# A hybrid decoder step on one core: even and odd columns in separate partitions for the block inverse, and old-state products in pairs

## The chip, the core and the metric

The kernel runs on one core of a Trainium2 chip. The metric is the device time of one execution in microseconds (us). A core has a matrix engine (PE, with its weight loads PEld), three engines for elementwise work (DVE, ACT, POOL) and a queue that issues transfers (SP). Each works through its own instructions in order and waits where an operand isn't ready.

## The reference

One inference step of one decoder layer for 256 prompt tokens and 8 sequences of 8 sample tokens. One input projection feeds a gated delta rule (mixer A) and a sparse attention with an indexer (mixer B); both are projected, gated, merged, projected again and normalised.

```python
h = rms_norm(x, pre_norm_g) * (1.0 + scale) + shift
(a_qkv, a_z, a_b, a_a, b_q, b_k, b_v, b_z, i_q, i_k, i_w, g_a, g_b) = split_columns(h @ w_in)
y_a, s_new, conv_new = gdn_branch(a_qkv, a_z, a_b, a_a, conv_buf, s0, ...)
y_b = attend(q, k, v, qi, i_w, i_k) * silu(b_z)
merged = sigmoid(g_a) * (y_a @ w_pa) + sigmoid(g_b) * (y_b @ w_pb)
return x + gate * rms_norm(merged @ w_out, post_norm_g), ...

# gdn_branch, for chunks of 64 tokens
a_strict = where(strict, (kb @ k.T) * decay, 0.0)
sol = triangular_solve(a_strict, rhs, lower=True, unit_diagonal=True)   # (1 + a_strict)^-1 rhs
u = u_c - w_c @ s                                    # the old state's part
o = qd_c @ s + qk_c @ u
s = s * gt_c + kt_c.T @ u
y = rms_norm(o, gdn_norm_g) * silu(z)
```

The sizes: width 2048, 16 query/key heads and 32 value heads of 128 in mixer A, 16 attention heads.

## The kernel before

All 320 tokens (256 prompt, 64 sample) stand as the moving side of PE, and the weights stream past them. Each weight block of 128x1024 arrives in `raw`, ACT rounds it to `whi`, DVE forms the rest `wlo = raw - whi`, and a main product is the sum of `xh,whi`, `xl,whi` and `xh,wlo`, 8 of each per block, accumulated in a bank `pm`. `whi` and `wlo` have three tiles each.

What else is computed is written as Python generators ("sides"). Between main matmuls a planner runs a round of sides (`side_round`). It keeps its own estimate of when each engine is done (`Clock`), and a side that yields a time is taken up again only when the estimate for PE has passed it: `ready(t)` is the estimate for t to be written, `idle(t)` for t to be written and read, `need(ring)` waits for a free buffer of a ring, and `force(cond)` runs sides until a condition holds. So an edit of a side changes the order of instructions far from it. Nearly all instructions are recorded by one helper and have line L64; they are told apart by the names of their tiles.

In order of time: the adaLN modulation and norm, to about 195 us; attention and indexer with their projections, to 690; gates, to 770; the recurrent stage, to 1650; the branch projections, to 1966; the output projection `stream_out`, to 2092; the last norm, to the end. The recurrent stage has 8 groups of two query/key heads (four value heads). A group has: convolution (`xp`, `cth`, `vf`, transposed by PE `ident,vf` into `vt`), the products `kq_gen`, one `inverse`, one `prompt_chain` and one `sample_chain` for each of its two heads, and a norm (six Squares `ps<-ot` on ACT for each head).

`inverse` inverts the unit triangular matrices of the group: 12 matrices of 128x128, cut into 48 blocks of 32x32 on the diagonal, one in each partition. The block's strict part is loaded into `blk`, `X` starts as the identity, and step j of 31 does two POOL instructions, `tmpx = blk[:, j, j+1:] x X[j, 0:j+1]` and `X[j+1:, 0:j+1] -= tmpx`. A copy puts the transposed inverse in `blk`; both forms are stored to `d_x` and loaded back as parts of `XT`, `X` and `blk`, and PE makes the off-diagonal blocks from them (first `ps<-X,blk`).

`sample_chain` multiplies the old states `S` (8 sequences) with the keys and queries in `R` (`ps<-S,R`, 16 instructions on PE), scales `S` by its decay on POOL (`S<-S,gtr`), subtracts the product from `vt` on DVE, and goes on with `ps<-vt,XT` and `ps<-w,ktok`.

At the end, `scaled(t, p, 3)` takes the sum of squares of the last quarter (ACT Square into `M`) and multiplies it by the gate (DVE); `root(t)` adds up and takes the power -1/2 (DVE, POOL `rs<-rs,mh`); `final(t)` does a multiply and add with the residual for four quarters (DVE) and stores each.

Of the kernel before, what the change touches and what calls it, by code (L numbers as in the profile page):

```python
# [16 lines left out]
D = 2048  # L17
# [212 lines left out]
class Kernel:  # L230
# [933 lines left out]
    def aux_gen(self):  # L1164
# [5 lines left out]
        for t, c0 in enumerate((0, 128, NT)):  # L1170
# [30 lines left out]
        rb = rbt[:, 0:256].rearrange("p (b h) -> p b h", b=NB)  # L1201
        self.tt(rb, self.rowb.rearrange("p (b o) -> p b o", o=1).to_broadcast([128, NB, 32]),
                g[:, 2:3, :].to_broadcast([128, NB, 32]), OP.mult)
        yield self.ready(g, rb)
        yield from self.need(self.ps_side, 2)
        p = self.psum()
        q = self.psum()
# [29 lines left out]
    def token_major(self, src, out_p, out_s, keep=None, keep_s=None):  # L1237

        nc = self.nc
        yield self.ready(src)  # L1240
        yield from self.need(self.ps_side)
        p = self.psum()
        for t in range(3):
            n = 128 if t < 2 else 64
            self.tr(p[:n, 128 * t:128 * t + 128], src[:, 128 * t:128 * t + n])
        if keep is None:
            yield from self.need(self.s_r)
            s = self.s_r.get()
# [12 lines left out]
    def ik_done(self, p):
# [478 lines left out]
    def gdn_open(self):  # L1740
# [15 lines left out]
        self.BT = Ring([a.tile([128, 12, 128], F32, name=f"BT{j}") for j in range(1)])  # L1756
        self.PT = Ring([b.tile([128, 2, 2, 128], F32, name=f"PT{j}") for j in range(3)])
        self.inv = Ring([(a.tile([128, 1024], F32, name="blk"), a.tile([128, 1024], F32, name="X"))])
        self.tmp = a.tile([48, 256], F32, name="tmpx")
        self.XT = Ring([b.tile([128, 12, 128], F32, name=f"XT{j}") for j in range(1)])  # L1760
        for t in self.ct.free:
            nc.gpsimd.memset(t, 0.0)
# [290 lines left out]
    def inverse(self, g, G):  # L2053
# [11 lines left out]
        yield from self.need(self.inv)  # L2065
        tiles = blk, Xt = self.inv.get()
        yield self.idle(blk, Xt)
        nc.sync.dma_start(blk[0:48], d_b.rearrange("k m j i -> (k m) (j i)"))
        nc.gpsimd.memset(Xt[0:48], 0.0)
        nc.gpsimd.memset(Xt[0:48, 0:1024:33], 1.0)  # L2070
        yield
        X = Xt[0:48].rearrange("p (i c) -> p i c", c=32)
        B = blk[0:48].rearrange("p (j i) -> p j i", i=32)
        for j in range(31):
            n, m = 31 - j, j + 1
            t = self.tmp[:, 0:n * m].rearrange("p (i c) -> p i c", c=m)
            bv = B[:, j, j + 1:32].rearrange("p (i o) -> p i o", o=1).to_broadcast([48, n, m])
            xv = X[:, j:j + 1, 0:m].to_broadcast([48, n, m])
            self.tt(t, bv, xv, OP.mult, eng=nc.gpsimd)
            self.tt(X[:, j + 1:32, 0:m], X[:, j + 1:32, 0:m], t, OP.subtract, eng=nc.gpsimd)  # L2080
            if j % 4 == 4 - 1:
                yield self.clock.last - 3.6
        nc.gpsimd.tensor_copy(blk[0:48].rearrange("p (c i) -> p c i", i=32), X.rearrange("p i c -> p c i"))
        yield
        while not self.XT.free:
            yield
# [4 lines left out]
        BO = blk[:, 0:512].rearrange("p (m c) -> p m c", c=64)  # L2091
        BD = blk[:, 512:768].rearrange("p (m c) -> p m c", c=32)
        Q1 = blk[:, 768:1024].rearrange("p (m c) -> p m c", c=32)
        nc.sync.dma_start(d_x[0].rearrange("k m i c -> (k m) (i c)"), Xt[0:48])
        nc.sync.dma_start(d_x[1].rearrange("k m i c -> (k m) (i c)"), blk[0:48])
        yield max(self.clock.last, self.idle(XT))
        nc.gpsimd.memset(XB[0:32, :, 32:64], 0.0)
        nc.gpsimd.memset(XE[32:64, :, 0:32], 0.0)
# [177 lines left out]
    def sample_chain(self, h, G):  # L2276
        nc, i, o = self.nc, self.i, self.o
        e, hv, K = h % 2, 2 * h, self.K[h]
        R = K["R"]
        yield from self.need(self.S)  # L2280
        S = self.S.get()
        yield self.idle(S)
        for v in range(2):
            nc.sync.dma_start(S[:, :, v, :], i["state_gdn"][0, :, hv + v].rearrange("b k v -> k b v"))
        while "T" not in G or "vt" not in K:
            yield
        vt, kt, XT = K["vt"], K["ktok"], G["XT"]
        s, stl = self.scal(G, e)
        yield self.ready(S, vt, XT)
        yield from self.need(self.ps_side)  # L2290
        yield from self.need(self.w)
        xr, wt = vt[:, 2], self.w.get()
        p = self.psum()
        for pp in range(2):
            for j in range(4):
                self.mm(p[32 * j:32 * j + 32, 0:256], R[:, 1 + pp, 32 * j:32 * j + 32], S[:, 2 * j + pp],
                        start=(pp == 0), stop=(pp == 1), skip=True)
        self.R.put(R)
        self.tt(S, S, self.gtr[:, :, hv:hv + 2].rearrange("p b (v o) -> p b v o", o=1).to_broadcast([128, NB, 2, 128]),
                OP.mult, eng=nc.gpsimd)  # L2300
        for v in range(2):
            self.stt(xr[:, v, :], p[:, 128 * v:128 * v + 128], self.neG[:, 2, hv + v:hv + v + 1], vt[:, 2, v, :],
                     OP.mult, OP.add)
        self.ps_side.put(p)
        yield
        yield from self.need(self.ps_side)
        if "ot" not in K:
            yield from self.need(self.ot)
            K["ot"] = self.ot.get()
        ot = K["ot"]  # L2310
        p = self.psum()
        for v in range(2):
            self.mm(p[:, 128 * v:128 * v + 128], XT[:, 8 + 2 * e + v, :], xr[:, v, :])
        self.act(ot[:, 2], p[:, 0:256].rearrange("p (v d) -> p v d", v=2))
        self.tt(wt, p[:, 0:256].rearrange("p (v d) -> p v d", v=2), stl(2), OP.mult)
        self.ps_side.put(p)
        self.drop_T(G)
# [147 lines left out]
        self.flags.add(flag)  # L2465

    def pb_open(self):
        self.force(lambda: self.chains == 16 and len(self.zf.free) == 4 and len(self.w.free) == 6
                   and len(self.gr.free) == 4)
        self.shut("gdnb")  # L2470
        a = self.open("merge", side="right")
        self.M, self.sga, self.sgb = (a.tile([128, KB, NT], F32, name=n) for n in ("M", "sga", "sgb"))
        self.stg.put(a.tile([128, NT], F32, name="stg2"))
        x = a.tile([128, KB, 2, NS], F32R, name="xs")
        self.xs = [x[:, k] for k in range(KB)]

        def gates():
            for src, dst, n in ((self.d_sigb, self.sgb, 10.0), (self.d_siga, self.sga, 20.0)):
                for k in range(0, KB, 2):
                    self.nc.sync.dma_start(dst[:, k:k + 2, :], src[k:k + 2].rearrange("k p t -> p k t"))  # L2480
                    self.gated += 2
                    yield self.later(n if k else 0.0)
        self.gated = 0
        g = gates()
        next(g)
        self.spawn(g, first=True)
        self.pt = Ring([a.tile([128, NT], F32, name=f"pt{j}") for j in range(2)])
        self.spawn(self.load_half(self.d_ya, 0, (self.xh, self.xl), "ya0"))

    def pb_done(self, p, k):  # L2490
        if k == 0:
            self.first = p
            return True
        if k == 1:
            self.pb_open()
            self.ps_main.put(self.psum())
            self.pb_sum(self.first, 0)
            self.ps_main.put(self.first)
        self.pb_sum(p, k)

    def pb_sum(self, p, k):
# [65 lines left out]
    def stream_out(self, u0):  # L2567
# [53 lines left out]
        def sample(p, w, kb, k, **kw):  # L2621
            product(p, self.xs[kb].rearrange("p e t -> p (e t)"), w[:, k], kb, **kw)

        def scaled(t, p, cg):
            c = slice(512 * cg, 512 * cg + 512)
            q = self.sq[t][:, cg:cg + 1]
            if t == 2:
# [76 lines left out]
        scaled(0, p0, 3)
        root(0)
        scaled(2, p, 3)
        root(2)
# [50 lines left out]
```

## Time and profile before

| what | before |
|---|---|
| median of 3 runs | 2102.92 us (2102.68 to 2103.71) |
| profiled execution: its time | 2101.78 us |
| profiled execution: its span | 2100.1 us |
| matmul instructions | 17409 |
| granted clock of PE, mean | 0.999 |
| main memory read | 388.38 MB |
| transferred over the span | 210 GB/s mean |

An instruction row has start and length in us, the engine, the operation, out<-in, the shape and how many follow each other; square brackets name the idle time ahead of it and what ended it. Idle time of an engine off the path costs nothing. The profiled execution's own span leaves out what lies before the first and behind the last instruction, 1.7 us.

### The profile page before, as it was taken

How to read it: one execution, taken by the hardware profiler on the slowest of the kernel's cores; microseconds unless marked ns; L12 is line 12 of the kernel's file. 1: busy time of each engine (PE TensorE's matmuls, PEld its weight loads, DVE VectorE, ACT ScalarE, POOL GpSimd, SP SyncE). 2: the span in 40 equal slices, each digit the busy share in tenths (PEclk: the TensorE clock that was granted, in tenths of full speed). 3: DMA queues.
4: the chain of work that ended last, by engine and by line, in shares of the span. 5: the costliest groups of instructions: out<-in, count | busy, mean ns of one | idle time of the engine just before them, and what ended most of it. 6: DMA issues, size and time to landing. Idle time of an engine off the chain costs nothing.

```text
span 2100.1 us, 44340 instructions
## 1 busy us (share of the span) xinstructions
PE 2080.3 (99%) x17409; PEld 1995.4 (95%) x17409; DVE 1358.0 (65%) x2541; ACT 986.9 (47%) x2213; POOL 567.8 (27%) x768
## 2 busy tenths in 40 slices
PE   8999999999999999999999999999999999999998
PEld 7999999999999999899999999999999999999986
DVE  5676648899855466676777676767666545445543
ACT  4225343333334356574747574747445534333431
POOL 1001000000010118484738383838471000000000
PEclk9999999999999999999999999999999999999999
DMA  9996758885686767696968686868697977575651
GB/s 346 347 345 192 195 146 259 238 261 153 186 260 211 216 164 201 152 257 148 253 160 249 158 242 165 237 163 243 160 260 207 257 208 213 167 182 149 198 193 51
DMA packets 693795, 440.65 MB, mean 210 GB/s; under 512 B 74209, under 2 KB 667985, under 8 KB 691281
## 3 DMA queue, kind: packets, MB, share of 16 engines
q1 hardware_dynamic: 689504, 415.15, 70.2%
q0 software_dynamic: 3616, 21.02, 2.8%
q8 instruction: 137, 2.24, 0.4%
q10 hardware_dynamic: 464, 1.65, 0.2%
q14 instruction: 74, 0.60, 0.1%
HBM read 388.38 MB, written 49.01 MB: 208 GB/s over the span
## 4 chain that ended last, share of the span: by engine, by line
PE 96%; DMA 2%; DVE 1%; issue 0%; ACT 0%; POOL 0%; DVEq 0%; POOLq 0%; ACTq 0%
PE pm L64 70%; PE ps L64 26%; DMA raw<-in_w_ada_dram 1%; DMA rawx<-in_w_ada_dram 1%; DMA c<-in_c_sample_dram 0%; DVE wlo L64 0%; POOL rs L64 0%; DVE awl L64 0%; DVE hT L64 0%; ACT M L64 0%; DVE sgb L64 0%; DVEq L2754 0%; DVE c L64 0%; DVE S L64 0%; DVE sga L64 0%
## 5 line engine op out<-in xcount | busy, mean ns | idle before, releaser
L64 PE MATMUL pm<-xh,whi 128*128 128x320 f32 (+1 forms) x2940 | 888.5, 317 | 0.7 <-DVE qiS L64 0.7
L64 PE MATMUL pm<-xl,whi 128*128 128x320 f32 (+1 forms) x2940 | 859.8, 307 | 0.3 <-DVE xl L64 0.2
L64 DVE TENSOR_TENSOR wlo<-raw,whi 128x1024 fp32r<-128x1024 f32 x446 | 574.8, 1294 | 248.0 <-ACT whi L64 215.8
L64 PEld LDWEIGHTS pm<-xh,whi 128*128 128x128 f32 x2940 | 552.9, 188 | 22.3 <-issue 17.3
L64 ACT ACTIVATE whi<-raw 128x1024 fp32r<-128x1024 f32 x446 | 467.8, 1056 | 192.2 <-PE pm L64 121.0
L64 PEld LDWEIGHTS pm<-xl,whi 128*128 128x128 f32 x2940 | 553.4, 188 | 1.5 <-DVE xl L64 0.7
L64 PE MATMUL pm<-xh,wlo 128*128 128x320 f32 (+1 forms) x2940 | 493.4, 307 | 0.5 <-DVE wlo L64 0.5
L64 PEld LDWEIGHTS pm<-xh,wlo 128*128 128x128 f32 x2940 | 443.8, 188 | 1.0 <-DVE wlo L64 1.0
L64 POOL TENSOR_TENSOR tmpx<-blk,X 48x31 f32<-48x31 f32 (+15 forms) x248 | 167.2, 674 | 45.3 <-DMA blk<-d_b 28.6
L64 POOL TENSOR_TENSOR X<-X,tmpx 48x31 f32<-48x31 f32 (+15 forms) x248 | 172.1, 694 | 19.4
L64 DVE SCALAR_TENSOR_TENSOR ps<-xp,cs,ps 128x344 f32<-128x344 f32 x192 | 111.5, 581 | 35.0 <-ACT ps L64 29.8
L64 POOL TENSOR_TENSOR rs<-rs,mh 128x1 f32<-128x1 f32 (+1 forms) x3 | 4.1, 1366 | 454.6 <-DVE rs L64 454.6
L64 POOL TENSOR_TENSOR S<-S,gtr 128x2048 f32<-128x2048 f32 x16 | 60.9, 3808 | 156.9 <-issue 97.8
L64 PE MATMUL pm<-y1h,whi 128*128 128x320 f32 x336 | 99.4, 308 | 0.0
L64 PE MATMUL pm<-y1l,whi 128*128 128x320 f32 x336 | 99.2, 307 | 0.0
L64 POOL DMA_INDIRECT a<-in_cache_k_dram,idx x8 | 7.5, 938 | 282.8 <-PE ps L64 267.8
L64 ACT ACTIVATE xp<-pm 128x256 f32<-128x256 f32 (+1 forms) x128 | 32.1, 303 | 110.1 <-PE pm L64 110.1
L64 ACT ACTIVATE vt<-ps,sc 128x128 f32<-128x128 f32 (+1 forms) x112 | 39.1, 412 | 54.3 <-PE ps L64 54.2
L64 PEld LDWEIGHTS pm<-y1l,whi 128*128 128x128 f32 x336 | 63.1, 188 | 0.0
L64 PEld LDWEIGHTS pm<-y1h,whi 128*128 128x128 f32 x336 | 62.8, 187 | 0.0
L64 ACT ACTIVATE t<-pm 128x320 f32<-128x320 f32 x36 | 15.9, 441 | 90.3 <-PE pm L64 90.2
L64 PE MATMUL pm<-y1h,wlo 128*128 128x320 f32 x336 | 56.1, 307 | 0.0
(463 smaller groups left out, 3081.7 us busy)
## 6 DMA issues: line engine op xcount, KB each, us to landing
raw<-in_w_in_dram SPq DMA_DIRECT2D x328, 512.0 KB
raw<-in_w_pa_dram SPq DMA_DIRECT2D x64, 512.0 KB
rawx<-in_w_ada_dram SPq DMA_DIRECT2D x18, 1024.0 KB
a<-in_w_ada_dram SPq DMA_DIRECT2D x16, 1024.0 KB
S<-in_state_gdn_dram SPq DMA_DIRECT2D x32, 512.0 KB
out_dram<-S SPq DMA_DIRECT2D x32, 512.0 KB
raw<-in_w_pb_dram SPq DMA_DIRECT2D x32, 512.0 KB
raw<-in_w_out_dram SPq DMA_DIRECT2D x32, 512.0 KB
```

What stands on the lines that cost most here:

```text
L64: made = fn(*args, **kw)
```

## The change

Five places of the program differ.

1. `inverse`: the 32 columns of each block are split; even columns stand in partitions 0 to 47, odd ones in 64 to 111. Each step handles `j // 2 + 1` columns on 112 partitions instead of `j + 1` on 48. `blk` is loaded into both halves; at the end two copies on POOL and two on DVE put the two forms together.
2. `sample_chain`: the first of a group's two chains only enters itself in a list; the second one issues both old-state products into one bank, both `S<-S,gtr` and the four subtractions, and then releases both.
3. `aux_gen` and `token_major`: 2 us are added to a time that is waited for, and a staging buffer is given back 4 us after its estimated last use.
4. `pb_open`, `pb_done`: up to four sums of the attention branch's projection wait in their banks for the end of the last chains, where two did, and the gate tiles for those are loaded without pauses.
5. `stream_out`: `root` comes between the Square and the gate product; `final` takes the quarters in the order 512, 1024, 0, 1536, and for the last 128 prompt tokens the quarter at 0 goes to ACT (Copy with scale) and POOL (add).

```diff
+            yield self.idle(s) + 4.0                  # token_major
             self.s_r.put(s)
...
-        self.tmp = a.tile([48, 256], F32, name="tmpx")
+        self.tmp = a.tile([112, 144], F32, name="tmpx")
...
-        nc.sync.dma_start(blk[0:48], d_b.rearrange("k m j i -> (k m) (j i)"))
-        nc.gpsimd.memset(Xt[0:48], 0.0)
-        nc.gpsimd.memset(Xt[0:48, 0:1024:33], 1.0)
+        for o in (0, 64):
+            nc.sync.dma_start(blk[o:o + 48], d_b.rearrange("k m j i -> (k m) (j i)"))
+        nc.gpsimd.memset(Xt[0:112, 0:512], 0.0)
+        for e, o in enumerate((0, 64)):
+            nc.gpsimd.memset(Xt[o:o + 48, 16 * e:512:33], 1.0)
...
-            n, m = 31 - j, j + 1
+            n, m = 31 - j, j // 2 + 1
...
-        nc.gpsimd.tensor_copy(blk[0:48].rearrange("p (c i) -> p c i", i=32), X.rearrange("p i c -> p c i"))
+        for e, o in enumerate((0, 64)):
+            x = X[o:o + 48]
+            nc.gpsimd.tensor_copy(blk[0:48].rearrange("p (i c e) -> p e i c", c=16, e=2)[:, e], x)
+            nc.vector.tensor_copy(blk[64:112].rearrange("p (c e i) -> p e i c", e=2, i=32)[:, e], x)
...
+        pair = G.setdefault("SR", [])
+        pair.append((hv, R, S, vt))
+        if len(pair) == 2:
+            yield self.ready(XT, *(x for _, _, a, b in pair for x in (a, b)))
+            p = self.psum()
+            for c, (_, r, sv, _) in zip((0, 256), pair):
+                for pp in range(2):
+                    for j in range(4):
+                        self.mm(p[32 * j:32 * j + 32, c:c + 256], r[:, 1 + pp, 32 * j:32 * j + 32], sv[:, 2 * j + pp], ...)
+                self.R.put(r)
+            for c, (h0, _, sv, vv) in zip((0, 256), pair):
+                self.tt(sv, sv, self.gtr[...], OP.mult, eng=nc.gpsimd)
+                for v in range(2):
+                    self.stt(vv[:, 2, v, :], p[:, c + 128 * v:c + 128 * v + 128], ...)
+            G["xr"] = True
+        while "xr" not in G:
+            yield
...
             self.act(out, src, AF.Square, accum_out=q)
+            if then:
+                then(t)
...
-            for c0 in range(0, D, 512):
+            for c0 in (512, 1024, 0, 1536):
...
+                if c0 == 0 and t == 1:
+                    self.act(g, g, AF.Copy, scale=r)
+                    self.tt(g, g, self.resid[t][:, c], OP.add, eng=nc.gpsimd)
+                else:
+                    self.stt(g, g, r, self.resid[t][:, c], OP.mult, OP.add)
```

PE executes the same instructions in number and kind, in another order. On PE, in the first group, the old-state products stood like this before (`ps_` are banks, `vt,XT` and `w,ktok` products of the chains, `X` parts of the inverse):

```order
L64 MATMUL ps_68<-X 64x64
L64 MATMUL ps_69<-XT_7835,X 64x64
L64 MATMUL ps_68<-X 64x64
L64 MATMUL ps_70<-vt_7838,XT_7835 128x128 x2
L64 MATMUL ps_71<-S_7849,R_7811 32x256 x8
L64 MATMUL ps_67<-vt_7839,XT_7835 128x128 x2
L64 MATMUL ps_69<-S_7850,R_7812 32x256 x8
L64 MATMUL ps_68<-w_7840,ktok_7815 128x256
```

and after:

```order
L64 MATMUL pm_65<-xl,whi_79 128x320
L64 MATMUL pm_65<-xh,wlo_82 128x320 x8
L64 MATMUL ps_67<-vt_7840,XT_7837 128x128 x2
L64 MATMUL ps_69<-vt_7841,XT_7837 128x128 x2
L64 MATMUL ps_68<-S_7851,R_7811 32x256 x8
L64 MATMUL ps_68<-S_7852,R_7812 32x256 x8
L64 MATMUL pm_65<-xh,whi_80 128x320
L64 MATMUL pm_65<-xl,whi_80 128x320
```

The two products follow each other into one bank, in every group; in the later groups of before, main matmuls stood between them.

On ACT, in the second group's convolution, the Squares of the two heads of the first group stood like this before (`ps,sc<-ot`; a later instruction scales `ot` in place):

```order
L64 ACTIVATE ps_72<-xp_7803,cs_102 128x344
L64 ACTIVATE ot_7846<-ot_7846,sc_7853 128x128 x6
L64 ACTIVATE ps_70,sc_7853<-ot_7847 128x128 x6
L64 ACTIVATE whi_79<-raw_75 128x1024
L64 ACTIVATE cth_7804<-ps_72 128x344
L64 ACTIVATE whi_80<-raw_75 128x1024
```

and after:

```order
L64 ACTIVATE vt_7840<-ps_67,sc_7854 128x256 x2
L64 ACTIVATE vt_7840<-ps_69,sc_7854 128x256
L64 ACTIVATE xp_7803<-pm_65 128x256
L64 ACTIVATE xp_7803<-pm_65 128x8x8
L64 ACTIVATE xp_7803<-cs_103 128x8x3
L64 ACTIVATE ps_72<-xp_7803,cs_103 128x344
L64 ACTIVATE ps_68,sc_7855<-ot_7848 128x128 x6
L64 ACTIVATE whi_78<-raw_76 128x1024
L64 ACTIVATE ps_71,sc_7856<-ot_7849 128x128 x6
L64 ACTIVATE whi_79<-raw_76 128x1024
L64 ACTIVATE cth_7804<-ps_72 128x344
```

Both heads' Squares now stand between `vt` and `cth`. On PE, the transposes that follow from this `cth` stand behind 48 main matmuls, counted from the transposes that release `vt`. Before, in the same convolution:

```order
L64 MATMUL pm_65<-xl,whi_78 128x320
L64 MATMUL pm_65<-xh,wlo_81 128x320 x8
L64 MATMUL ps_68<-ident,vf_7819 128x128 x2
L64 MATMUL ps_67<-ident,vf_7819 128x128
L64 MATMUL ps_68<-ident,vf_7820 128x128 x2
L64 MATMUL ps_67<-ident,vf_7820 128x128
L64 MATMUL pm_65<-xh,whi_79 128x320
```

and after:

```order
L64 MATMUL pm_66<-xh,wlo_83 128x320 x8
L64 MATMUL ps_70<-ident,ct_7806 128x128
L64 MATMUL ps_67<-ident,vf_7819 128x128 x2
L64 MATMUL ps_69<-ident,vf_7819 128x128
L64 MATMUL ps_67<-ident,vf_7820 128x128 x2
L64 MATMUL ps_69<-ident,vf_7820 128x128
L64 MATMUL pm_65<-xh,whi_78 128x320
```

The transposes of `ct` and `vf` now stand in one burst, half a block earlier against the Squares. At the end of the program DVE had before:

```order
L64 SCALAR_TENSOR_TENSOR sga<-sga,rs_21288,M 128x512 x4
L64 SCALAR_TENSOR_TENSOR sgb<-sgb,rs_21290,sga 64x512 x4
L64 TENSOR_TENSOR sgb<-ps_69,sgb 128x512
L64 TENSOR_SCALAR rs_21289<-sq_21286,rs_21289 128x1
L64 SCALAR_TENSOR_TENSOR sgb<-sgb,rs_21289,M 128x512 x4
```

and after:

```order
L64 SCALAR_TENSOR_TENSOR sga<-sga,rs_21330,M 128x512 x4
L64 SCALAR_TENSOR_TENSOR sgb<-sgb,rs_21332,sga 64x512 x4
L64 TENSOR_SCALAR rs_21331<-sq_21328,rs_21331 128x1
L64 TENSOR_TENSOR sgb<-ps_72,sgb 128x512
L64 SCALAR_TENSOR_TENSOR sgb<-sgb,rs_21331,M 128x512 x3
```

The sum for the root now stands ahead of the gate product, and three quarters are left to DVE.

More of the change, by code (lines that the diff above doesn't have):

```diff
@@ L1203, in aux_gen @@
                 g[:, 2:3, :].to_broadcast([128, NB, 32]), OP.mult)
-        yield self.ready(g, rb)
+        yield self.ready(g, rb) + 2.0
         yield from self.need(self.ps_side, 2)
@@ L1758, in gdn_open @@
         self.inv = Ring([(a.tile([128, 1024], F32, name="blk"), a.tile([128, 1024], F32, name="X"))])
-        self.tmp = a.tile([48, 256], F32, name="tmpx")
+        self.tmp = a.tile([112, 144], F32, name="tmpx")
+        for t in self.inv.free[0]:
+            nc.gpsimd.memset(t, 0.0)
         self.XT = Ring([b.tile([128, 12, 128], F32, name=f"XT{j}") for j in range(1)])
@@ L2067, in inverse @@
         yield self.idle(blk, Xt)
-        nc.sync.dma_start(blk[0:48], d_b.rearrange("k m j i -> (k m) (j i)"))
-        nc.gpsimd.memset(Xt[0:48], 0.0)
-        nc.gpsimd.memset(Xt[0:48, 0:1024:33], 1.0)
+        for o in (0, 64):
[3 more added lines that the diff above has]
+            nc.gpsimd.memset(Xt[o:o + 48, 16 * e:512:33], 1.0)
         yield
-        X = Xt[0:48].rearrange("p (i c) -> p i c", c=32)
-        B = blk[0:48].rearrange("p (j i) -> p j i", i=32)
+        X = Xt[0:112, 0:512].rearrange("p (i c) -> p i c", c=16)
+        B = blk[0:112].rearrange("p (j i) -> p j i", i=32)
         for j in range(31):
-            n, m = 31 - j, j + 1
+            n, m = 31 - j, j // 2 + 1
             t = self.tmp[:, 0:n * m].rearrange("p (i c) -> p i c", c=m)
-            bv = B[:, j, j + 1:32].rearrange("p (i o) -> p i o", o=1).to_broadcast([48, n, m])
-            xv = X[:, j:j + 1, 0:m].to_broadcast([48, n, m])
+            bv = B[:, j, j + 1:32].rearrange("p (i o) -> p i o", o=1).to_broadcast([112, n, m])
+            xv = X[:, j:j + 1, 0:m].to_broadcast([112, n, m])
             self.tt(t, bv, xv, OP.mult, eng=nc.gpsimd)
@@ L2093, in inverse @@
         Q1 = blk[:, 768:1024].rearrange("p (m c) -> p m c", c=32)
-        nc.sync.dma_start(d_x[0].rearrange("k m i c -> (k m) (i c)"), Xt[0:48])
-        nc.sync.dma_start(d_x[1].rearrange("k m i c -> (k m) (i c)"), blk[0:48])
+        nc.sync.dma_start(d_x[0].rearrange("k m i c -> (k m) (i c)"), blk[0:48])
+        nc.sync.dma_start(d_x[1].rearrange("k m i c -> (k m) (i c)"), blk[64:112])
         yield max(self.clock.last, self.idle(XT))
@@ L2288, in sample_chain @@
         s, stl = self.scal(G, e)
-        yield self.ready(S, vt, XT)
-        yield from self.need(self.ps_side)
-        yield from self.need(self.w)
[L2292 to L2305, printed above, removed]
+        xr = vt[:, 2]
+        pair = G.setdefault("SR", [])
+        pair.append((hv, R, S, vt))
+        if len(pair) == 2:
+            yield self.ready(XT, *(x for _, _, a, b in pair for x in (a, b)))
+            yield from self.need(self.ps_side)
+            p = self.psum()
+            for c, (_, r, sv, _) in zip((0, 256), pair):
+                for pp in range(2):
+                    for j in range(4):
+                        self.mm(p[32 * j:32 * j + 32, c:c + 256], r[:, 1 + pp, 32 * j:32 * j + 32], sv[:, 2 * j + pp],
+                                start=(pp == 0), stop=(pp == 1), skip=True)
+                self.R.put(r)
+            for c, (h0, _, sv, vv) in zip((0, 256), pair):
+                self.tt(sv, sv, self.gtr[:, :, h0:h0 + 2].rearrange("p b (v o) -> p b v o", o=1).to_broadcast(
+                    [128, NB, 2, 128]), OP.mult, eng=nc.gpsimd)
+                for v in range(2):
+                    self.stt(vv[:, 2, v, :], p[:, c + 128 * v:c + 128 * v + 128], self.neG[:, 2, h0 + v:h0 + v + 1],
+                             vv[:, 2, v, :], OP.mult, OP.add)
+            self.ps_side.put(p)
+            G["xr"] = True
+            yield
+        while "xr" not in G:
+            yield
+        yield self.ready(xr)
+        yield from self.need(self.w)
+        wt = self.w.get()
         yield from self.need(self.ps_side)
@@ L2467, in pb_open @@
     def pb_open(self):
-        self.force(lambda: self.chains == 16 and len(self.zf.free) == 4 and len(self.w.free) == 6
-                   and len(self.gr.free) == 4)
+        self.force(self.chain_end)
         self.shut("gdnb")
@@ L2475, in pb_open @@
         self.xs = [x[:, k] for k in range(KB)]
+        self.gated = 0
+        opened = len(self.pend)
         def gates():
@@ L2481, in gates @@
                     self.gated += 2
-                    yield self.later(n if k else 0.0)
-        self.gated = 0
+                    if self.gated > opened + 1:
+                        yield self.later(n if k else 0.0)
         g = gates()
@@ L2488, in pb_open, with chain_end @@
         self.spawn(self.load_half(self.d_ya, 0, (self.xh, self.xl), "ya0"))
+    def chain_end(self):
+        return (self.chains == 16 and len(self.zf.free) == 4 and len(self.w.free) == 6 and len(self.gr.free) == 4)
     def pb_done(self, p, k):
         if k == 0:
-            self.first = p
-            return True
-        if k == 1:
-            self.pb_open()
-            self.ps_main.put(self.psum())
-            self.pb_sum(self.first, 0)
-            self.ps_main.put(self.first)
+            self.pend = []
+        if self.pend is not None:
+            self.pend.append((p, k))
+            if len(self.pend) < 4 and not self.chain_end():
+                self.force(lambda: self.ps_side.free)
+                self.ps_main.put(self.psum())
+                return True
+            self.pb_open()
+            pend, self.pend = self.pend, None
+            for b, j in pend:
+                self.pb_sum(b, j)
+                if j < k:
+                    self.ps_main.put(b)
+            return
         self.pb_sum(p, k)
@@ L2622, in sample, with scaled @@
             product(p, self.xs[kb].rearrange("p e t -> p (e t)"), w[:, k], kb, **kw)
-        def scaled(t, p, cg):
+        def scaled(t, p, cg, then=None):
             c = slice(512 * cg, 512 * cg + 512)
@@ L2654, in final @@
             dst = self.o[0][0, 128 * t:128 * t + 128] if t < 2 else self.o[1].rearrange("b t d -> (b t) d")
-            for c0 in range(0, D, 512):
+            for c0 in (512, 1024, 0, 1536):
                 c = slice(c0, c0 + 512)
                 g = self.scaled[t][:, c]
-                self.stt(g, g, r, self.resid[t][:, c], OP.mult, OP.add)
+                if c0 == 0 and t == 1:
[3 more added lines that the diff above has]
+                    self.stt(g, g, r, self.resid[t][:, c], OP.mult, OP.add)
                 nc.sync.dma_start(dst[:, c], g)
@@ L2703, in stream_out @@
             before(t)
[L2704 to L2707, printed above, removed]
+        scaled(0, p0, 3, root)
+        scaled(2, p, 3, root)
         final(0)
@@ L2718, in stream_out @@
         self.force(lambda: not self.sides)
-        scaled(1, p1, 3)
-        root(1)
+        scaled(1, p1, 3, root)
         final(1)
```

## The prediction

> **What bounds the kernel now.** I read the page's busy shares and its chain first, then the busy time by stretches of 100 us, then what TensorE (PE) waited for, and last the single instructions at the places that the change touches.
>
> ```profile
> PE 2080.3 (99%) x17409; PEld 1995.4 (95%) x17409; DVE 1358.0 (65%) x2541; ACT 986.9 (47%) x2213; POOL 567.8 (27%) x768
> PE 96%; DMA 2%; DVE 1%; issue 0%; ACT 0%; POOL 0%; DVEq 0%; POOLq 0%; ACTq 0%
> ```
>
> PE is busy for 2080.3 of 2100.1 us and the chain that ended last is PE for 96%. So only three things move the end: time on PE itself, gaps on PE, and what lies behind its last matmul. The gaps by stretch (the third column is PE's busy time and its matmuls):
>
> ```profile
> 0.00:100.00 100.00, 90.55 (x1132) 84.04 (x1136) 59.96 (x163) 36.15 (x55) 10.18 (x33) 1.00 1.05 349
> 800.00:900.00 100.00, 99.02 (x813) 94.02 (x812) 66.72 (x143) 58.10 (x155) 65.71 (x90) 1.00 0.68 177
> 1500.00:1600.00 100.00, 99.53 (x836) 94.53 (x835) 56.78 (x96) 49.93 (x120) 58.03 (x75) 1.00 0.78 209
> 1700.00:1800.00 100.00, 100.00 (x684) 100.00 (x683) 50.50 (x66) 36.94 (x45) 0.00 (x0) 1.00 0.68 197
> 2000.00:2100.00 100.00, 91.94 (x398) 74.34 (x396) 41.11 (x55) 28.46 (x45) 4.10 (x3) 0.97 0.34 111
> PE ps L64 <- DVE S L64: 0.5, 1, 0.5
> PE ps L64 <- ACT XT L64: 0.5, 1, 0.5
> PE pm L64 <- DVE c L64: 7.5, 2, 7.2
> ```
>
> Start (9.45 us without PE) and end (8.06) are the big gaps; the diff leaves the start alone. In the recurrent stage there are 0.98 us in 800 to 900 and 0.47 in 1500 to 1600, together 1.45. Nothing there waits for POOL. The stretch 1700 to 1800 is full: 684 matmuls in 100 us, 0.146 us for each main matmul (320 columns).
>
> **The change, part by part.**
>
> *Substitution on even and odd columns.* 62 POOL instructions per inverse, eight inverses:
>
> ```profile
> L64 POOL TENSOR_TENSOR tmpx<-blk,X 48x31 f32<-48x31 f32 (+15 forms) x248 | 167.2, 674 | 45.3 <-DMA blk<-d_b 28.6
> L64 POOL TENSOR_TENSOR X<-X,tmpx 48x31 f32<-48x31 f32 (+15 forms) x248 | 172.1, 694 | 19.4
> 1006.55 0.62 POOL L64 TENSOR_TENSOR tmpx<-blk,X 48x256 f32<-48x256 f32 x1
> 1007.24 1.67 POOL L64 TENSOR_TENSOR X<-X,tmpx 48x256 f32<-48x256 f32 x1
> 1253.19 0.23 POOL L64 TENSOR_TENSOR tmpx<-blk,X 48x31 f32<-48x31 f32 x1
> 1253.82 2.08 POOL L64 COPY blk<-X 48x1024 f32<-48x1024 f32 x1
> ```
>
> Before, (167.2 + 172.1) / 8 = 42.4 us per inverse. The slope is (0.62 - 0.23) / 225 elements = 1.7 ns an element. The work falls from 5456 to some 2850 elements per chain of operations, 92 a piece instead of 176: 0.23 + 61 x 0.0017 = 0.33 us each, 21 us for 62. The rows give no price for 112 partitions against 48; I take the same, and 42.4 (no gain) as the other end. Some instructions take 1.0 us more than their length asks (1007.24: 1.67), and that I leave per inverse as it is, some 7 us. So about 28 us, some 14 saved per inverse. On the end this is worth nothing: PE waits for no POOL row, and the planner spends the shorter time by placing later steps earlier. The permuting copy of 2.08 us becomes two of half the size on POOL and two on DVE, which has 35% of its time free: nothing. If that cover were gone, 2 x some 0.6 us would stand ahead of a weight's low half in each group, 10 us in all; the low halves run ahead of PE (the third rival says how far).
>
> The second load of `blk` adds one issue to SP per inverse. The loads behind it:
>
> ```profile
> 1165.16 0.46 SPq L64 DMA_DIRECT2D X<-d_x  x1
> 1167.99 0.69 PE L64 MATMUL ps<-X,blk 32*32 32x32 f32 x32
> ```
>
> One issue is 0.46 us. The last X load left SP at 1165.62 and PE used it at 1167.99, 2.4 us later; 0.46 us fit. In the new order, in the second group, the same product stands behind its loads by less, 0.6 us in main matmuls: a wait from 0 to 2 us there. I take 0.5 for this and the like of it.
>
> *Old-state products in pairs.*
>
> ```profile
> 1071.69 1.07 PE L64 MATMUL ps<-S,R 128*32 128x256 f32 x16
> 1072.69 0.42 PE L64 MATMUL pm<-xh,whi 128*128 128x320 f32 x1
> 1072.94 0.31 PE L64 MATMUL pm<-xl,whi 128*128 128x320 f32 x1
> 1075.97 1.07 PE L64 MATMUL ps<-S,R 128*32 128x256 f32 x16
> 1076.97 0.41 PE L64 MATMUL pm<-xh,whi 128*128 128x320 f32 x1
> ```
>
> Each product takes 1.00 us to the next main matmul, and the first main matmul behind it 0.25 instead of 0.146, 0.10 too much. Paired, one such return falls away per group, 0.8 us in eight; a change of shape at the head, which the rows don't price apart, may save up to 0.15 more, 2.0 us in all. The instructions on PE are the same in number, but other side products have new neighbours too. Between 0 (everything given back by new neighbours; there are 282 bursts of side work instead of 279) and -4.4 (each row of the new order at the mean distance which that pair of kinds has in this trace) I take -3.0, near the pairs' own price with one unit for the neighbours.
>
> *Where the new order makes PE wait.* With both chains of a group released together, both of its norm bursts on ACT come one behind the other, and the next convolution's rows stand behind them.
>
> ```profile
> 994.23 1.21 ACT L64 ACTIVATE vt<-ps,sc 128x256 f32<-128x256 f32 x3 [3.17 <-PE ps L64]
> 996.46 0.26 ACT L64 ACTIVATE ps<-ot 128x128 f32<-128x128 f32 x1
> 998.93 1.04 ACT L64 ACTIVATE whi<-raw 128x1024 fp32r<-128x1024 f32 x1
> 999.88 0.44 ACT L64 ACTIVATE cth<-ps 128x344 f32<-128x344 f32 x1
> 1257.31 1.21 DVE L64 TENSOR_TENSOR wlo<-raw,whi 128x1024 fp32r<-128x1024 f32 x1
> 1287.49 0.54 DVE L64 SCALAR_TENSOR_TENSOR vf<-cth,ps 128x256 f32<-128x256 f32 x2
> 1530.71 0.55 PE L64 MATMUL ps<-ident,vf 128*128 128x128 f32 x3 [0.47 <-DVE S L64]
> ```
>
> After the first group's chains the new ACT order is: `vt`, the convolution's copies, six Squares, `whi`, six Squares, `whi`, `cth`. By the rows: 996.46 - 994.23 = 2.23 to the Squares; 998.93 - 996.46 = 2.47 for six; 0.95 for a `whi`; 2.47 and 0.95 again: 9.07. Then DVE does `wlo` (1.21) and the pair `vf` (0.54): with handovers about 11.0 us after `vt` began. PE releases that `vt` by its transposes and has 48 main matmuls (7.0 us) and some 0.4 us of transposes before it needs `vf`: 7.4. So PE waits 3.6 us, where the longest such wait before was 0.47. Ends: 2.5, if ACT is early at the first Square, and 4.5, if `wlo` is stretched. The waits of before, 1.45 us, stood in the same products at other places and go.
>
> *Store slots, the late sums of the branch projection, gate loads.* They shift transfers and side work in stretches like 1700 to 1800, where PE has no gap to give. Nothing; the bound for moved transfers is one issue, 0.46 us, per step.
>
> *The end.*
>
> ```profile
> 2092.53 0.19 ACT L64 ACTIVATION_READ_ACCUMULATOR M<-ps 128x1 f32 x1
> 2092.76 0.69 DVE L64 TENSOR_TENSOR sgb<-ps,sgb 128x512 f32<-128x512 f32 x1 [2.81 <-ACT M L64]
> 2093.37 0.20 DVE L64 TENSOR_SCALAR rs<-sq,rs 128x1 f32<-128x1 f32 x1
> 2093.65 0.56 POOL L64 TENSOR_TENSOR rs<-rs,mh 128x1 f32<-128x1 f32 x1 [6.47 <-DVE rs L64]
> 2094.25 2.74 DVE L64 SCALAR_TENSOR_TENSOR sgb<-sgb,rs,M 128x512 f32<-128x512 f32 x4 [0.67 <-POOL rs L64]
> ```
>
> All of this is on the path, after PE's last matmul. The power on POOL now runs beside the gate product: 94.25 - 93.65 = 0.60 less. One of four quarters of 0.69 goes to ACT and POOL: at best 0.7 less again, if they work beside DVE. At worst nothing or less, if POOL's add stops DVE:
>
> ```profile
> 1287.06 3.62 POOL L64 TENSOR_TENSOR S<-S,gtr 128x2048 f32<-128x2048 f32 x1 [24.56 <-issue]
> 1287.95 3.82 DVE L64 TENSOR_TENSOR wlo<-raw,whi 128x1024 fp32r<-128x1024 f32 x1
> ```
>
> Here DVE's `wlo`, 1.21 alone, ended 1.09 us after POOL's multiplication had ended: it did nothing until then. POOL's add of a quarter should be a quarter of 3.62 and a base, about 1.0 us. Stopping DVE for that long costs 0.3 more than the quarter that was saved. So the end lies between -1.3 and -0.3; I take -0.6, since this row is the nearest.
>
> The Trainium skill, "SBUF — State Buffer", section "Who interferes with whom", says the same of the end's two operations: a VectorE instruction with two SBUF inputs and a GpSimd instruction that reads SBUF exclude each other for a whole instruction. By it the quarter moved to POOL gains nothing and the end is worth 0.3; without it 1.3.
>
> **Sum.** PE's order -3.0, the new `vf` wait +3.6, other new waits +0.5, old waits -1.45, the end -0.6: -0.95 us. The profiled execution took 2101.78 (its span 2100.1), 1.14 under the median of 2102.92; taken from the median, 2102.0. A measurement of this kernel can tell about 0.2%, 4.2 us, from no change.
>
> **Rivals.** *Faster* (0.27): the `vf` wait doesn't appear, because ACT meets the second `ot` late enough to do `whi` and `cth` first or PE itself comes later. Then PE's order counts up to -4.4, old waits -1.45, the end -1.3: 2095.8. For it: before has the same Squares in every group, and its longest wait of this kind is 0.47. Against it: the order on ACT is fixed, and the burst stands ahead of `cth`.
>
> *It does nothing that reaches the end* (0.09): the substitution is off PE's path and the pairs save nothing; only the end's 0.6 stays: 2102.3. For it: no wait for POOL in the list. Against it: PE's rows have a price, 0.10 at each return.
>
> *Slower* (0.14): two `S<-S,gtr` of 3.62 stand back to back on POOL in every group, and a `wlo` that waits is passed over by the second. Before, the two were 4.2 us apart. The low halves are kept in three tiles, each good for 24 main matmuls, 3.5 us; two finished ones give PE 7.0 us of cover. A `wlo` that stands behind both and then runs takes 3.6 + 3.6 + 1.2 = 8.4, so PE waits 1.4 us a group. In all eight: 11.2 - 0.95, 2113.2; from four groups on (5.6 - 0.95 = 4.65) it is measurably slower. Against it speaks this row:
>
> ```profile
> 1254.56 2.43 DVE L64 TENSOR_TENSOR wlo<-raw,whi 128x1024 fp32r<-128x1024 f32 x1 [0.78 <-ACT whi L64]
> ```
>
> It waited for the copy that ended at 1255.90 and then ran, though POOL's next instruction was ready: DVE came in after one. The same section of the Trainium skill has the one that starts first hold the pair for its whole instruction, which doesn't say who is next.
>
> **How the numbers follow.** My forecast has 0.50; it lies within 4.2 us of the median, with its own range from 2098.8 (PE's order -4.4, `vf` 2.5, the end -1.3) to 2106.5 (PE's order 0, `vf` 4.5, X waits 2). The faster rival has 0.27, of which half is between 2096 and 2098.7. With half of the slower one above 2107.5 that range holds 8 in 10: 2096 to 2107.5. Faster by over 0.2%: 0.27; within: 0.50 + 0.09 = 0.59; slower: 0.14.
>
> **What would show it.** Right: POOL's two substitution groups together near 230 us for 496; two S,R products in one burst of about 1.9 us with one slow main matmul behind; PE's longest wait in the recurrent stage at a `ps<-ident,vf` in the second group, 2.5 to 4.5 us; POOL's power beginning before DVE's gate product ends; stt rows in the last 5 us longer than 0.69 while POOL adds. Wrong: PE's waits in the stage sum to under 1 us (faster), or `PE pm <- DVE wlo` becomes the largest row of the waits (slower).

## The result: 0.8% slower

The changed kernel takes 2118.86 us (median of 6 runs, 2115.6 to 2120.19), before 2102.99 (6 runs, 2100.05 to 2105.14): ratio 1.0077, 95% interval 1.0066 to 1.0088. The forecast was 2102.0, in a range that ended at 2107.5. The page of the profile after, its busy line and its chain:

```profile
PE 2084.2 (98%) x17409; PEld 2003.2 (95%) x17409; DVE 1345.2 (64%) x2556; ACT 986.5 (47%) x2214; POOL 469.5 (22%) x787
PE 85%; POOL 7%; DVE 2%; issue 2%; DMA 2%; ACT 1%; SPq 0%; DVEq 0%; POOLq 0%; ACTq 0%
```

POOL, which had 0% of the chain that ended last, has 7% of it now, although its busy time fell by 98 us. The stretches of the recurrent stage (PE's busy time third, PE's granted clock in the third column from the end) and PE's waits (us in total, how often, the longest):

```profile
800.00:900.00 100.00, 93.79 (x771) 89.71 (x770) 65.13 (x143) 56.73 (x159) 43.86 (x72) 0.97 0.64 173
1200.00:1300.00 100.00, 97.67 (x788) 94.87 (x787) 65.74 (x142) 58.93 (x158) 49.93 (x82) 0.98 0.74 197
1300.00:1400.00 100.00, 97.38 (x801) 93.76 (x800) 62.58 (x128) 60.95 (x168) 49.60 (x87) 0.98 0.81 214
1400.00:1500.00 100.00, 97.21 (x757) 94.91 (x755) 68.31 (x145) 60.35 (x165) 45.10 (x86) 0.98 0.73 194
PE ps L64 <- DVE R L64: 6.5, 3, 3.0
PE pm L64 <- DVE wlo L64: 5.5, 4, 2.6
PE ps L64 <- DVE vf L64: 3.2, 1, 3.2
```

Six waits of 0.7 to 3.2 us make 14.7 us in the stage, against 1.45 us of gaps before, and the clock is below 1.00 in stretches where it was 1.00. The waits name DVE. What DVE waited for stands in its own rows (instruction rows of the changed kernel, DVE, POOL and PE around 1244):

```profile
1235.54 1.44 DVE L64 TENSOR_TENSOR wlo<-raw,whi 128x1024 fp32r<-128x1024 f32 x1
1243.78 1.60 DVE L64 COPY blk<-X 48x512 f32<-48x512 f32 x2 [6.79 <-POOL X L64]
1243.52 0.22 POOL L64 TENSOR_TENSOR X<-X,tmpx 112x16 f32<-112x16 f32 x1
1246.05 1.60 DVE L64 TENSOR_TENSOR wlo<-raw,whi 128x1024 fp32r<-128x1024 f32 x1
1247.71 1.45 PE L64 MATMUL pm<-xh,wlo 128*128 128x320 f32 x8 [2.33 <-DVE wlo L64]
```

The two new copies stand at the head of DVE's queue and wait 6.79 us for the last substitution step on POOL. Behind them stand `kq`, `R` and the next `wlo`; PE has used up its finished weights by then and waits 2.33 us. The answer for the copies in all eight groups:

```profile
L64 DVE COPY blk<-X x16: 591/775/999, 822.4 to 1573.8; 48x512 f32<-48x512 f32 x16
  POOL X L64: 45.0, 8
```

DVE stood idle for 45.0 us ahead of them, 5.6 a group. The copies are put in DVE's order together with the last substitution steps, and the generator takes those up 3.6 us ahead of its estimate of POOL (`yield self.clock.last - 3.6`). The same lead stood there before the change, but then only POOL's own instructions came under it, and PE waited for no POOL row. Now two copies in DVE's queue come under it as well.

After a wait comes a second loss. PE in the changed kernel around the `vf` wait at 898.95:

```profile
898.95 0.90 PE L64 MATMUL ps<-ident,vf 128*128 128x128 f32 x3 [3.24 <-DVE vf L64]
899.50:904.50 5.00, 5.00 (x21) 5.00 (x20) 0.92 (x3) 4.80 (x14) 4.06 (x13) 0.50 0.85 237
904.50:908.00 3.50, 3.50 (x26) 3.50 (x26) 2.73 (x4) 3.21 (x9) 3.11 (x6) 1.00 0.41 101
```

For 5 us behind the wait the granted clock is 0.50: 21 matmuls where 34 main ones of 0.146 us would have run. Added up from the starts of main matmuls more than 0.147 us apart, the slow clock behind the five long waits costs 1.2 + 2.3 + 1.7 + 1.1 + 1.3 = 7.6 us, and it counts as busy time. (Main matmuls alone are counted, so the figure is rather low.)

So the 17.2 us between the two spans are: PE's idle time in the stage 14.9 - 1.45 = +13.5, of which the six waits make 14.7; busy time 2084.2 - 2080.3 = +3.9, which is +7.6 of slow clock and so -3.7 from the new order; the end -0.2. The idle time ahead of the stage is the same, 10.2 us in both.

### The profile page after: what moved, and what is told of

The parts are those of the page before. It is cut to its first block, busy times and chain, and to the rows that moved or that the text cites. A ratio compares the mean times of both kernels' runs of the same rounds, so it can differ in the third digit from the quotient of the medians.

```text
span 2117.3 us, 44356 instructions
## 1 busy us (share of the span) xinstructions
PE 2084.2 (98%) x17409; PEld 2003.2 (95%) x17409; DVE 1345.2 (64%) x2556; ACT 986.5 (47%) x2214; POOL 469.5 (22%) x787
## 4 chain that ended last, share of the span: by engine, by line
PE 85%; POOL 7%; DVE 2%; issue 2%; DMA 2%; ACT 1%; SPq 0%; DVEq 0%; POOLq 0%; ACTq 0%
PE pm L64 59%; PE ps L64 26%; POOL X L64 4%; POOL tmpx L64 3%; DMA blk<-d_b 1%; DVE wlo L64 1%; ACT ps L64 0%; DMA raw<-in_w_ada_dram 0%; SPq L64 0%; DVE ps L64 0%; DMA c<-in_c_sample_dram 0%; DMA d_ya<-zf 0%; DVE blk L64 0%; ACT whi L64 0%; ACT xp L64 0%
## 5 line engine op out<-in xcount | busy, mean ns | idle before, releaser
L64 DVE TENSOR_TENSOR wlo<-raw,whi 128x1024 fp32r<-128x1024 f32 x446 | 557.4, 1255 | 239.6 <-ACT whi L64 211.7
L64 POOL TENSOR_TENSOR tmpx<-blk,X 112x126 f32<-112x126 f32 (+22 forms) x248 | 117.3, 473 | 52.1 <-DMA blk<-d_b 33.4
L64 POOL TENSOR_TENSOR X<-X,tmpx 112x126 f32<-112x126 f32 (+22 forms) x248 | 117.2, 473 | 19.4
L64 POOL TENSOR_TENSOR sc<-sc,mh 128x6 f32<-128x6 f32 (+1 forms) x24 | 38.6, 1609 | 99.1 <-DVE sc L64 97.8
L64 ACT ACTIVATE t<-pm 128x320 f32<-128x320 f32 x36 | 15.8, 440 | 90.0 <-PE pm L64 89.9
```

Of the source, the lines that this page charges most:

```text
L64: made = fn(*args, **kw)
```

## The experiments

Theory A: the place of the DVE copies in an in-order queue, and the slow clock behind each wait. Theory B: POOL's work on 112 partitions. A third: the pairs stretch `wlo`. Times are medians of runs beside runs of before on the same chip (2102.73 for e1 to e4, 2101.89 for e5 to e7, 2101.16 for e9 and e11), ratios with 95% intervals.

**e1, all four copies on POOL.**

```diff
-            nc.vector.tensor_copy(blk[64:112].rearrange(...)[:, e], x)
+            nc.gpsimd.tensor_copy(blk[64:112].rearrange(...)[:, e], x)
```

> The changed kernel, but the two DVE copies at the end of each inverse are POOL copies (four on POOL). Theory A (DVE takes its instructions in order, so a copy that waits 5 to 8 us for POOL's substitution holds up wlo, R and kq behind it, PE starves for 2.3 to 3.0 us four times, and after each of these waits its clock is 0.5 for some 3 to 6 us): the waits of PE for R and wlo (12.0 us in all) go to under 1 us, and with them some 5 us of slow clock; the wait for vf (3.2 us, with 2.3 us of slow clock behind it) stays, since both bursts of Squares still stand two rows apart; about 2102 us. Theory B (the substitution on 112 partitions and its collisions with wlo on the shared port are what is late): the four copies make POOL's chain 2 us longer, the waits stay or grow, 2117 us or more.

2104.97 us, 1.001 (1.000 to 1.0019): 14 us less than the changed kernel though POOL does more. PE's waits:

```profile
PE ps L64 <- DMA X<-d_x: 3.3, 2, 2.5
PE ps L64 <- DVE vf L64: 3.2, 1, 3.2
```

The waits for R are gone, those for `wlo` are back at the 0.5 us of before, and `vf` stayed, as A has it; B is out. A's number was missed by 3 us: the last group has a new wait for the loads of `X`, 3.3 us, with some 1.6 us of slow clock behind it. The stores ahead of these loads now stand behind POOL's copies, which is the likely reason; no run separates it.

**e2, the DVE copies later in DVE's order.**

```diff
+        yield self.ready(X) + 1.0
+        for e, o in enumerate((0, 64)):
+            nc.vector.tensor_copy(blk[64:112].rearrange(...)[:, e], X[o:o + 48])
```

> The changed kernel, but the two DVE copies are placed in DVE's order only when the planner's estimate for the end of the substitution, plus 1 us, has passed. Theory A: DVE's idle time ahead of a copy falls from 5 to 8 us to under 2 us, PE's waits for R and wlo go, vf stays: about 2102 us. If the planner's estimate is several us early on the chip, a part of the idle time stays and the time lies between 2103 and 2110. Theory B: 2117 us or more.

2102.82 us, 1.000 (0.9991 to 1.0009). The same copies on the same engine, only placed later:

```profile
  POOL X L64: 11.0, 5
PE ps L64 <- DVE R L64: 1.5, 1, 1.5
```

DVE's idle time ahead of them fell from 45.0 to 11.0 us, and 16 us of the time with it. Of the waits for R and `wlo` one of 1.47 us remained, where the planner's estimate was early; it isn't followed by a slow clock. The `vf` wait stayed at 3.2 us, as A has it, and one of 0.8 us for the loads of `X` is new.

**e3, the inverse of before, all else as changed.** The diff is that of `inverse` and `tmpx` in the change, undone.

> The changed kernel with the inverse of before (48 partitions, 32 columns, one POOL copy); pairs, store slots and the end as changed. Theory A: no PE wait for R or wlo over 1 us; the bursts of Squares stand 19 rows apart, so no vf wait either; what stays is the gain of the order (PE busy 3.7 us less at full clock) and of the end (0.2): about 2098 us. Theory B gives the same here. A third theory, that the pairs hold up DVE (two S<-S,gtr back to back stretch a wlo), keeps the wlo waits of 2.3 and 2.6 us: 2108 us.

2097.9 us, 0.9971 (0.996 to 0.9982): the forecast of 2098, and faster than before. Busy time of PE on its page:

```profile
PE 2076.4 (99%) x17409; PEld 1995.9 (95%) x17409; DVE 1343.5 (64%) x2540; ACT 989.2 (47%) x2214; POOL 573.2 (27%) x769
```

PE is busy 3.9 us less than before, with a clock of 0.999. The rest of the change is worth 5 us. Putting the split inverse on top costs 21, the `vf` wait included: that wait is in the kernels which have both the split inverse and the pairs (the changed one, e1, e2), and neither here nor in e4, which has the split inverse alone.

**e4, the sample chain of before, all else as changed.** The diff is that of `sample_chain`, undone.

> The changed kernel with the sample chain of before (each chain issues its own old-state product); inverse, store slots and the end as changed. Theory A: the DVE copies still wait for POOL, so R and wlo waits of some 10 us with 5 us of slow clock stay; the Squares stand 8 rows apart, so the vf wait falls to under 1 us with its slow clock (5.5 us); the pairs' gain of 2 to 4 us goes: about 2116 us. The third theory (pairs stretch wlo): no wlo waits, 2106 us or less.

2126.58 us, 1.0102 (1.0086 to 1.0118). PE's waits:

```profile
PE pm L64 <- DVE wlo L64: 8.7, 6, 3.7
PE ps L64 <- DVE R L64: 8.3, 3, 5.1
```

The waits for `wlo` are larger without the pairs, so the third theory is out; `vf` is gone from the list. I expected 2116. The waits for R and `wlo` came to 17.0 us and not 10, at DVE's idle time of 46.4 us ahead of the copies, nearly that of the changed kernel. So how much of an idle DVE reaches PE depends on the order around it (e8 and e10 measure this).

**e5, e2 with the second head's Squares 5 us later.**

```diff
         yield self.ready(ot)
+        if e:
+            yield self.later(5.0)
```

> The kernel of e2 (DVE copies placed later), and the second head's Squares of each group wait 5 us longer in the planner, so that the two bursts stand 20 rows apart on ACT. If the vf wait comes from the two bursts ahead of cth, it falls from 3.2 us to under 0.5, the slow clock behind it (2.3 us) goes too, and the time falls from e2's 2102.8 to about 2097. If vf is late for another reason (DVE's wlo, POOL), the wait stays above 2 us and the time is 2102 to 2103.

2094.93 us, 0.9968 (0.9956 to 0.998). `vf` is gone from the waits, and the longest left in the stage is 0.5:

```profile
PE 2074.8 (99%) x17409; PEld 1995.1 (95%) x17409; DVE 1347.2 (64%) x2556; ACT 988.3 (47%) x2214; POOL 482.3 (23%) x787
PE ps L64 <- DVE R L64: 0.5, 1, 0.5
```

**e6, the pairs alone on the kernel before**, and **e11, the pairs with the changed `pb_open` and `pb_done`.** Both diffs are the change's own.

> The kernel before with the changed sample chain alone (old-state products in pairs). If e3's gain of 5 us is the pairs' shorter order on PE and the waits of before that go, this has nearly all of it: about 2098.5 us, PE busy 3 to 4 us less. If the gain comes from the store slots, the late sums or the end, this stays at 2102 to 2103.

> The kernel of e6 (before with the pairs) and the changed pb_open and pb_done, which let up to four sums of the attention branch's projection wait in their banks. If e6's wait of 3.2 us at its start comes from the two banks of before being taken while the chains end later, it goes here, with some 2 us of slow clock: about 2099 us. If it stays, the late sums are worth nothing and the time is 2104 to 2105.

e6: 2104.68 us, 1.0013 (1.0004 to 1.0022), so my number was missed. The pairs shorten PE's order (PE is busy 2.2 us less than before, with 1.5 us of slow clock in it), but the sums of the attention branch's projection now wait:

```profile
1655.41 0.61 PE L64 MATMUL pm<-y1h,whi 128*128 128x320 f32 x1 [3.19 <-DVE M L64]
```

The wait is 3.19 us. e11: 2098.75 us, 0.9987 (0.9978 to 0.9996): with four sums held back this wait is gone, some 5.5 us by the two ratios for an edit that I had costed at nothing. (e11's profiled execution has a wait of 2.9 us in the attention stage, for gathered rows, which the other profiles don't have; the median is the better figure.)

**e7, e3 with all four last quarters on DVE.**

```diff
-                if c0 == 0 and t == 1:
+                if c0 == 0 and t > 2:
```

> The kernel of e3, with all four last quarters multiplied and added on DVE; the root still comes ahead of the gate product. If POOL's add stops DVE for its length, the quarter on ACT and POOL gained nothing: from PE's last matmul to the span's end it is 7.5 us or less, against 7.9 in e3, and the time is about 2097.5 us (at or under e3, not to be told from it by the times alone). If they worked side by side, the end is 0.3 to 0.7 us longer than in e3.

2096.99 us, 0.9976 (0.9967 to 0.9985). The ends, of e3:

```profile
2089.39 3.08 DVE L64 SCALAR_TENSOR_TENSOR sgb<-sgb,rs,M 128x512 f32<-128x512 f32 x3
2090.19 1.74 POOL L64 TENSOR_TENSOR sgb<-sgb,M 128x512 f32<-128x512 f32 x1 [0.83 <-ACT sgb L64]
```

and of e7:

```profile
2089.37 2.74 DVE L64 SCALAR_TENSOR_TENSOR sgb<-sgb,rs,M 128x512 f32<-128x512 f32 x4
```

Three quarters with POOL beside them take longer than four alone. From PE's last matmul to the end of the span it is 7.91 us in e3 and 7.53 in e7, 8.16 before.

**e8 and e10, DVE held for known times.** e3, and in groups 1 to 7 so many writes of a scratch tile behind POOL's copy, outside the planner's books, so that the order is e3's but for them.

```diff
+        for _ in range((0, 6, 10, 14, 16, 18, 20, 24)[g]):     # e10: (0, 14, 12, 15, 10, 10, 10, 12)
+            nc.vector.engine.memset(self.hold, 0.0)
```

> The kernel of e3, and behind the substitution's POOL copy in groups 1 to 7 DVE writes a scratch tile 6, 10, 14, 16, 18, 20 and 24 times (some 2.6 to 10.3 us), which nothing reads and nothing waits for; the planner doesn't count them, so the order is otherwise e3's. Theory A (the place in DVE's queue is what costs, not what the copies do): no PE wait up to about 5 us of hold; from there a wait that grows with the hold, to 3 to 5 us at the longest; the clock falls to 0.5 behind waits of 2.3 us and more and stays at 1.0 behind waits under 1.5 us. If the hold alone does nothing (PE is starved by POOL's lateness or by the copies' port), no wait over 1 us in any group. The whole is one look, not timed.

> The kernel of e8 with other counts: 14, 12, 15, 10, 10, 10 and 12 writes (0.66 us each) in groups 1 to 7. If each microsecond of hold beyond a place's cover is a microsecond of PE's wait, the waits follow from e8's: group 2 1.32 + 2 x 0.66 = 2.6, group 3 2.05 + 0.66 = 2.7, group 4 5.19 - 6 x 0.66 = 1.2, group 5 6.49 - 8 x 0.66 = 1.2, group 6 7.94 - 10 x 0.66 = 1.3, group 7 8.49 - 12 x 0.66 = 0.6 us. Clock: 0.5 for some 4 to 6 us behind groups 2 and 3, 1.0 behind the others, if the length of the wait decides (none at 2.05 in e8, slow at 2.33 in the changed kernel); if the place in the program decides, it stays at 1.0 in groups 2 and 3 and falls in 4 to 7. One look, not timed.

The writes follow each other every 0.66 us (two rows of e8: 936.33 and 936.99), so a hold is 0.66 us times their number. Groups count from 0.

| group | e8 hold | e8 PE wait | e10 hold | e10 PE wait | hold less wait (e8, e10) |
|---|---|---|---|---|---|
| 1 | 4.0 | none | 9.2 | 1.73 | 7.5 |
| 2 | 6.6 | 1.32 | 7.9 | 2.56 | 5.3, 5.4 |
| 3 | 9.2 | 2.05 | 9.9 | 2.75 | 7.2, 7.2 |
| 4 | 10.6 | 5.19 | 6.6 | 1.25 | 5.4, 5.4 |
| 5 | 11.9 | 6.49 | 6.6 | 1.25 | 5.4, 5.4 |
| 6 | 13.2 | 7.94 | 6.6 | 1.38 | 5.3, 5.2 |
| 7 | 15.8 | 8.49 | 7.9 | 0.40 | 7.4, 7.5 |

Holding DVE does what the waiting copies did, so A's mechanism is shown. PE's cover against a held DVE is 5.2 to 7.5 us, set by the place, and each microsecond beyond it is one of PE's; e10's waits came within 0.2 us of what was expected. For e8 I had expected holds of 2.6 to 10.3 us and waits of 3 to 5 us at the longest; a write took longer than I had counted, the holds came to 4.0 to 15.8 us and the longest wait to 8.49. In both, some loads of `X` came late as well, up to 2.6 us, which nobody expected. On the clock e10 was half wrong: I expected it to fall behind groups 2 and 3 and nowhere else; it fell behind group 3, not behind group 2, and behind two late loads of `X`. Stretches behind its waits of 1.77 (in the small products `ps<-X,blk`), 2.56 and 2.75 us:

```profile
966.00:970.00 4.00, 4.00 (x18) 4.00 (x18) 2.01 (x4) 2.22 (x4) 0.00 (x0) 0.57 0.60 97
1056.60:1060.00 3.40, 3.27 (x23) 3.27 (x24) 3.40 (x9) 1.06 (x1) 0.00 (x0) 1.00 0.62 164
1167.00:1171.00 4.00, 3.85 (x16) 3.85 (x17) 3.93 (x13) 1.06 (x1) 2.55 (x4) 0.58 0.66 177
```

**e9, e5 with the last quarters of e7.**

> The kernel of e5 with all four last quarters on DVE, as in e7. If the quarter on ACT and POOL costs the 0.4 us that e7's end was shorter than e3's (7.53 against 7.91 from PE's last matmul), and nothing else changes, the end is 7.5 us and the time 2094.5 us, against 2094.9 in e5; faster than before by about 0.35%.

2094.43 us, 0.9966 (0.9954 to 0.9978), the fastest of all. Against e5 the 0.5 us can't be told from noise by the times; the span fell by 0.5 as well.

## Why the prediction was wrong

- **The step that failed** is the copies: "two of half the size on POOL and two on DVE, which has 35% of its time free: nothing". I priced their length (0.8 us each, as it came out) and not their wait. They need POOL's last step, so DVE's queue stands still from where they are placed until POOL is done, 5.6 us a group. A share of free time says nothing about what stands behind a waiting instruction. "If that cover were gone" priced 1.2 us a group, 10 us in all; moving the copies later, with nothing else, took 16 us off (e2). In the sum the copies stood at 0 and late loads of `X` at +0.5; measured are 11.5 us of waits for R and `wlo`, with 5.3 us of slow clock behind them, and no wait for `X`.
- **The slow clock** behind a wait was in no term. It took 7.6 us here, on top of 14.7 us of waits.
- **POOL's substitution** was right: 117.3 + 117.2 = 234.5 us for 496 instructions, forecast 230. The hit is in part luck: of the 42.4 us before, the prediction kept "some 7 us" as extra time of single instructions, but its own slope leaves 42.4 - 62 x 0.48 = 12.8; the runs showed 29.3 - 20.7 = 8.6. That it is off PE's path was true of POOL's rows and false once DVE waited for them.
- **The `vf` wait** was right in place and size: 3.6 forecast, 3.24 measured. ACT took 9.05 us from `vt` (888.16) to `cth` (897.21), 9.07 forecast. e5 shows the cause: with the Squares apart it is gone. The prediction put the two bursts down to the pairs alone; e3 has the pairs and not the wait. With its clock it cost 5.5 us, not 3.6.
- **PE's order**: -3.0 forecast, -3.7 to -3.9 measured (the changed kernel less its slow clock; e3). The -3.0 was chosen between 0 and -4.4, and its 0.15 us for a change of shape at the head is shown by no row or run.
- **The late sums** at nothing were wrong: alone the pairs bring a wait at 1655, and the late sums take it away (e6, e11). My reason, PE at 100% in that stretch before, held only as long as the chains ended when they did.
- **The end**: -0.6 forecast, -0.2 measured, beyond the bound of -0.3, which the prediction had worked out from the row that it called the nearest. The early root gave its 0.60 (PE's end to the first `stt`: 2.31 before, 1.71 after), and the quarter on ACT and POOL took 0.4 back (e7). The exclusion that the Trainium skill states in "SBUF — State Buffer", section "Who interferes with whom", agrees with the trace: DVE's three took 3.08 us while POOL's add ran (1.74), 1.0 more than three of e7's four (2.06).
- **The slower rival** named another instruction, the doubled `S<-S,gtr`. e4 and e3 exclude it: with pairs and no copies on DVE no `wlo` wait is over 0.3 us.
- **The range**: its upper end doesn't follow from its terms. PE's order 0, `vf` 4.5 and `X` waits 2 are 3.0, 0.9 and 1.5 us above the terms of the forecast, which gives 2102.0 + 5.4 = 2107.4 and not 2106.5. The measured time is beyond both.

## What to carry to other kernels

When work moves to an engine with free time, ask what the moved instruction waits for and what stands behind it in that queue; the price is the wait beyond the cover, not the length. Here the planner's lead of 3.6 us did no harm while only POOL's own instructions came under it, and cost 16 us where two copies in DVE's queue came under it as well. And price a gap on the matrix engine with the slow clock behind it: here the 2.3 to 3.2 us of each long wait cost 1.1 to 2.3 more.

## What the hardware showed that I had not expected

The granted clock falls to 0.50 behind most waits of over 2.3 us. In the stage, waits of 1.25 to 1.5 us left it at 1.0 (five of them), so did ones of 1.73, 2.03, 2.05 and once 2.56 us; from 2.6 up it always fell, at 2.33 and 2.47 too, and once at 1.77, in the middle of small 32x32 products. So length alone does not decide.

The traces show what does. Ahead of the end of the program every slow stretch in them lasts 3.41, 6.83 or 10.24 us, and the stretches at full clock between two slow ones are whole multiples of 3.41 us too (68.27 us, 20 times, between the first two of the changed kernel). So the clock changes only on a grid of 3.41 us, which lies elsewhere against the program in each trace. Windows on this grid, first around the wait of 2.33 us in the changed kernel, then around the wait of 2.56 us in e10:

```profile
1245.81:1249.22 3.41, 1.51 (x10) 1.51 (x11) 3.34 (x8) 2.48 (x3) 3.20 (x7) 1.00 0.15 43
1249.22:1252.63 3.41, 3.41 (x15) 3.41 (x14) 3.41 (x8) 2.69 (x10) 3.34 (x4) 0.50 0.90 277
1051.56:1054.97 3.41, 2.61 (x19) 2.34 (x17) 2.51 (x6) 1.36 (x2) 1.57 (x1) 1.00 0.00 0
1054.97:1058.38 3.41, 1.65 (x11) 1.65 (x12) 3.27 (x5) 1.06 (x1) 0.00 (x0) 1.00 0.11 21
1058.38:1061.79 3.41, 3.41 (x28) 3.41 (x27) 3.31 (x12) 0.00 (x0) 0.00 (x0) 1.00 0.95 259
```

The shorter wait leaves PE idle for 1.90 us of one window (3.41 - 1.51), and the next one is slow. The grid cuts the longer wait into 0.80 and 1.76 us, and the clock stays. Over all 13 traces, behind the first 30 us and ahead of the last matmul, each window at full clock with 1.90 us or more of idle PE was followed by a slow one, and each with up to 1.76 us was not; between them 1.89 us (e8) was not and 1.77 us (around the 32x32 products) was. A slow window was followed by another slow one where PE was idle for 0.77 us or more, and by a fast one up to 0.52 us. The Trainium skill, "TensorE: Matmul & The Clock Gate", section "Part 1: The HAM clock gate (the "warmup" mystery)", tells of an activity window of about 3.4 us that runs freely and of a clock halved after an idle window. The grid agrees with that. If the window is meant to be idle throughout, the traces differ: 1.90 of 3.41 us were enough here.
